# Output projection of a two-layer encoder trunk: a buffer of its own for y's weight sum, h's sum on a reloaded block, row sums of m1 and m2 put behind v's

## The chip, the cores and the metric

The kernel runs on one core of a Trainium2 chip. The metric is the device time of one execution in microseconds (us), the median of the timed runs. A second, profiled execution gives the trace; its times are counted from the start of its span.

## What is computed

Two layers, each a token mixer with three branches and then a feed-forward net (FFN), on 512 rows of width 1024 in float32. The change touches the output projection that closes the mixer and the layer norm behind it:

```
mix = jnp.einsum('bsd,de->bse', merged, w_out[l])            # 512x1024 by 1024x1024
x = _layer_norm(DEEPNORM_ALPHA * x + mix, ln1_g[l], ln1_b[l])
u = jnp.einsum('bsd,df->bsf', x, w_ffn_in[l])                # the FFN's first product
```

## The kernel before

**Products.** A float32 operand is carried as a pair of float32r parts, hi and lo. A product of two pairs takes three matmuls: hi by hi (L122), lo of one by hi (L123), hi by lo (L124). Weights are split after they are loaded: ScalarE (ACT) casts the hi part (L287 for a block of 128x2048; L154 for the FFN's and others' 128x1024), and VectorE (DVE) subtracts it from the loaded block to get lo (L288, L155).

**Seven products in place of eight.** The output projection is a Strassen-Winograd scheme on 512x512 blocks of `w_out`. Write W00, W01, W10, W11 for the blocks. Seven products, in the order m1, m2, y, v, x, g, h, use the weight blocks W00 (m1), W10 (m2), W00+W01 (y), W11 (v), W00+W01+W11 (x), W01+W11 (g) and W00+W01+W11+W10 (h). The left operands are sums of blocks of the merged activations (tiles `m1*`, `m2*`, `s12*`, `s43*`; L310, L311, L320 and L321 form them on DVE, L108 on ACT and L114 on DVE split them). `product` (L367) works one of them for two row tiles j = 0, 1 with 4 blocks k and 3 matmuls each: 24 matmuls of 128x512 each. x and g are added in PSUM onto m1's banks, h too, and v onto y's banks.

**Row sums.** The residual stream lies in tiles `z`, one for each row tile t and column half hf. `plus` (L1157) adds a finished PSUM bank to z on DVE: L1165 the first time (it scales z too), L1167 afterwards; with `final` it takes the statistics of the layer norm right behind it (L494). When both halves of a row tile have theirs, `normalise` follows: L511 and L513 on DVE, a power on GpSimd (POOL, L514), and L516 on DVE. Transposes on the TensorE (PE, L534 into `px`) turn z; ACT scales it (L550) and casts it (L106), DVE makes its lo part (L112), and the result `xT` feeds the FFN.

**Weight sums.** A load is a DMA of 1 MB issued from SyncE (SP, L174) into one of four staging buffers `st`. W00 is loaded into buffer `a` for m1. Behind m1's split an accumulating DMA (L178, issued from POOL) adds W01 onto `a`: y's block. For v, W11 is loaded into a buffer `d`, and DVE adds it onto `a` (L226): x's block. Behind x's split a second accumulating DMA adds W10 onto `a`: h's block. g's sum is made in a buffer `c` ahead of time, with an accumulating DMA of its own.

**What sets the order.** A list of items (L1215 to L1245) says in which order weight blocks are needed and which side work (`s_mleft`, `s_mright`, `s_turned`) goes with each. An item's weights are fetched up to three blocks ahead of its matmuls, since there are three buffers each for `wh` and `wl`. A tile scheduler then places each engine's instructions in one fixed order, and each engine works its own list strictly in that order. So does the DMA queue of SP. Both layers hold the same sequence here.

Of the kernel before, what the change touches and what calls it, by code (L numbers as in the profile page):

```python
# [56 lines left out]
def trunk(ctx, tc, x_in, xT_in, w_in, ret_norm_g, da_norm_g, lq1, lk1, lq2, lk2, w_a, w_b, w_c, b_merge, w_out,  # L57
          ln1_g, ln1_b, w_ffn_in, w_ffn_out, ln2_g, ln2_b, rel, rope_ret, rope_da, decay, out):
    nc = tc.nc
# [131 lines left out]
    class Chain(Halves):  # L191
# [12 lines left out]
        def y(self):  # L204
            return self.take(1, 1)

        def x(self):
            return self.take(1, 0)
# [4 lines left out]
        def v(self):  # L213
            return self.block(self.load(1, 1))

        def h(self):
            return self.block(self.__dict__.pop("a"))

    class Mixed(Chain):

        def v(self):
            self.d = self.load(1, 1)
            b = self.block(self.d)
            nc.vector.tensor_add(self.a, self.a, self.__dict__.pop("d"))  # L226
            return b

        def x(self):
            return self.take(1, 0)  # L230

        def y(self):
            return self.block(self.a)

    class Close(Halves):

# [130 lines left out]
    def product(acts, name, j, wt, ps=None):  # L367

        onto, sl = ps is not None, slice(P * j, P * j + P)
        ps = ps if onto else bank("pf")  # L370
        for k in range(wt.nk):
            hi, lo = acts[k].use[name]
            mm3(ps, hi[:, sl], lo[:, sl], wt.hi[:, k], wt.lo[:, k], k == 0 and not onto, k == wt.nk - 1, onto)
        return ps
# [257 lines left out]
    def layer(l):  # L632
# [7 lines left out]
        v = {}  # L640
# [421 lines left out]
        mq = {}  # L1062
# [32 lines left out]
        def u_branch(br, i):  # L1095
            w = (w_a, w_b, w_c)[br][l]
            nk = w.shape[0] // P

            def fn(wt):
                act = (oa, ob, oc)[br]  # L1100
                for j, d in enumerate(tiles(br, i)):
                    t = th.pop((br, d))
                    if br == 0:
                        away, t = t, g(name="th")
                        nc.sync.dma_start(t, away)
                    ps = proj_T(act, wt, P * j, nk=nk)
                    nc.vector.scalar_tensor_tensor(t, t, 1.0, ps, op0=ALU.add, op1=ALU.mult)
                    if br == 0:
                        acc[d] = t
                    else:  # L1110
                        nc.vector.tensor_add(acc[d], acc[d], t)
                    if br == 2 and j == 0:
                        q = mq[d] = Quarters()
                        pr = HalfPair("m1")
                        split(pr, acc[d][:, q.A], scale=0.5)
                        q.put("m1", pr, q.A)
                    elif br == 2:
                        pr = Pair("m2")
                        split(pr, acc[d], scale=0.5)
                        mq[d - 4].put("m2", pr, q.A)  # L1120
                        mq[d - 4].put("h", pr, q.B)
                    between()
            return [(cols_of(w, 0, br, i), nk)], fn
# [26 lines left out]
        x1 = {}  # L1150
# [9 lines left out]
        def plus(x, t, hf, ps, op, final=False):  # L1160

            z = x["z"][t][hf]
            if (t, hf) in x["fresh"]:
                x["fresh"].remove((t, hf))
                nc.vector.scalar_tensor_tensor(z, z, ALPHA, ps, op0=ALU.mult, op1=op)  # L1165
            else:
                nc.vector.tensor_tensor(z, z, ps, op=op)  # L1167
            if final:
                x["n"].stats(t, hf)
# [7 lines left out]

        def out_items():

            hv = Mixed(w_out[l], 0, 4)  # L1180
            w = {}

            def it(name, i, hf, op, last=False, whole=False):
                def fn(wt):
                    on = {"x": "m1", "g": "m1", "h": "m1", "v": "y"}.get(name, name)
                    for j in range(2):
                        t = 2 * i + j
                        w[on, j] = product(mq, name, j, wt, w.pop((on, j), None))
                        plus(x1, t, hf, w[on, j], op, last)
                        if name in ("m2", "v", "h"):  # L1190
                            w.pop((on, j))
                        if whole:
                            x1["n"].normalise(t)
                        between()
                return [getattr(hv, name)], fn

            add, sub = ALU.add, ALU.subtract
            return {"c": hv.ahead_c, "m1": it("m1", 0, 0, add), "m2": it("m2", 0, 0, add, True), "y": it("y", 1, 1, add),
                    "x": it("x", 0, 1, sub, True, True), "v": it("v", 0, 1, add), "g": it("g", 1, 1, sub, True),
                    "h": it("h", 1, 0, add, True, True)}  # L1200

        def s_turned(hf):
# [7 lines left out]
        o = out_items()  # L1210
# [15 lines left out]
        for (specs, fn), *groups in start + [  # L1226
            (w["x"], [p["a"]]), (u_gate(0, 3),), (w["g"],), (w["h"], [p["c"]]),
            (p["m1"], [s_dh(0)]), (p["y"], [], [s_r1(0)]), (p["v"], [s_dh(1)]), (p["m2"], [], [s_r1(1)]),
            (p["x"], [q["a"]]), (u_rqk(rq, RQ, 1),), (p["g"], [q["c"]]), (p["h"],),
            (q["m1"], [], [s_r2(0)]), (q["y"], [s_r2(1)]), (u_rqk(rk, RK, 1), [], [s_r3(0)]),  # L1230
            (q["v"], [s_dh(2)], [s_r3(1)]), (q["m2"], [], [s_r1(2)]), (q["x"], [s_dh(3)]), (u_cqk(0), [], [s_r1(3)]), (q["g"],), (q["h"],),
            (u_gate(2, 0), [s_r2(2)], [s_r2(3), s_r3(2)]), (u_cqk(1), [s_r3(3)] + c(0)[0], c(0)[1]),
            (u_branch(0, 0), c(1)[0] + [v_back(cv)], c(1)[1]), (u_branch(0, 1), *c(2)), (u_cqk(2), *c(3)),
            (u_branch(0, 2), *c(4)), (u_cqk(3), *c(5)), (u_branch(0, 3), *c(6)), 
            (u_dqk(0), [s_c3(5), s_c2(6)], [s_c1(7)]), (u_gate(1, 0), [s_c3(6)], [s_c2(7)]),
            (u_dqk(1), [v_back(dv), s_c3(7)] + d(0)[1]), (u_branch(1, 0), *d(1)),
            (u_gate(1, 1), [], d(2)[1]), (u_branch(1, 1), [s_d2(0)], d(3)[1]), (u_dqk(2), [s_d3(0)]),
            (u_gate(1, 2), *d(4)), (u_branch(1, 2), *d(5)), (u_dqk(3),),
            (u_gate(1, 3), *d(6)), (u_branch(1, 3), *d(7)), (u_gate(2, 1), [gates_in(2, 0), s_d4(2)], [s_d2(3)]),
            (u_gate(2, 2), [s_d3(3)], [rows_in, s_d4(3)]),  # L1240
            (u_branch(2, 0), [], [s_mleft(0)]), (u_branch(2, 1), [], [s_mleft(1)]), (u_gate(2, 3), [s_mright(0)], [s_mright(1)]),
            (u_branch(2, 2), [o["c"]]), (u_branch(2, 3), [], [s_mleft(2), s_mleft(3)]),
            (o["m1"], [s_mright(2)]), (o["m2"], [s_mright(3)]), (o["y"],), (o["v"],), (o["x"], [norm_rows]),
            (o["g"], [], [s_turned(0)]), (o["h"],),
        ]:  # L1245
            item(specs, fn, *groups)
# [237 lines left out]
```

## Time and profile before

| what | value |
|---|---|
| timed runs, median (lowest to highest) | 1887.76 us (1886.77 to 1888.65) |
| profiled execution, its own time | 1890.11 us |
| its span in the trace | 1888.3 us |
| PE busy | 1860.3 us, 99% of the span |
| DVE busy | 1392.3 us, 74% |
| ACT busy | 989.1 us, 52% |
| granted TensorE clock, mean | 0.996 |

The span is from the first instruction to the last; the execution's own time has 1.8 us around it. A row of the timeline gives the start, the length, the engine, the line and the operation, then what it writes and reads. A bracket at its end gives the idle time ahead of it on that engine and what ended it. Matmuls overlap: one of 128x512 is shown with 0.39 us, and the next starts 0.23 us later. The output projection lies at about 545 to 604 us in the first layer and 1486 to 1544 us in the second.

### The profile page before, as it was taken

Reading aid. Unit: us, or ns where it says so; the run is one execution under the profiler, and the core shown is the slowest. Engines: PE = TensorE matmul, PEld = TensorE weight load, DVE = VectorE, ACT = ScalarE, POOL = GpSimd, SP = SyncE. Lnnn points to the kernel's source line nnn. Section 1 sums busy time; section 2 is a strip of 40 time slices with the busy share of each in tenths; the row PEclk is TensorE's granted clock in tenths of the full one; section 3 lists DMA queues with packets and bytes.
Section 4 is the critical chain, followed back from the end, with each engine's and each line's share of the span. In section 5 each row is a group of like instructions: output and inputs, shape, how many; then the busy total and the mean of one; then the engine's idle time right before and its main releaser. Section 6 shows DMA issues by size and latency. Waiting matters only on the chain. (4 is left out here: it accounts for less than half of the span.)

```text
span 1888.3 us, 23317 instructions
## 1 busy us (share of the span) xinstructions
PE 1860.3 (99%) x8754; PEld 1547.7 (82%) x8754; DVE 1392.3 (74%) x2119; ACT 989.1 (52%) x1593; POOL 133.7 (7%) x151
## 2 busy tenths in 40 slices
PE   9999999999999999999999999999999999999998
PEld 7788888888877888788878888888888778888886
DVE  6777756677578776889587777567775887778886
ACT  5545545576544544555264555546665454455541
POOL 2000000000001000010020000000000011000100
PEclk9999999999999999999999999999999999999999
DMA  9585444232357677697486844533323576777871
GB/s 291 165 268 152 123 145 124 90 125 77 121 136 174 160 187 192 164 230 198 145 218 183 258 126 123 164 115 100 113 68 123 134 200 148 197 193 203 203 195 45
DMA packets 234881, 300.79 MB, mean 159 GB/s; under 512 B 8724, under 2 KB 127600, under 8 KB 234768
## 3 DMA queue, kind: packets, MB, share of 16 engines
q1 hardware_dynamic: 205488, 242.25, 39.3%
q0 software_dynamic: 29280, 57.05, 17.7%
q8 instruction: 69, 1.13, 0.3%
q14 instruction: 44, 0.36, 0.1%
HBM read 277.20 MB, written 22.07 MB: 158 GB/s over the span
## 5 line engine op out<-in xcount | busy, mean ns | idle before, releaser
L288 DVE TENSOR_TENSOR wl<-st,wh 128x2048 fp32r<-128x2048 f32 x140 | 320.1, 2289 | 124.2 <-ACT wh L287 123.6
L287 ACT CAST wh<-st 128x2048 fp32r<-128x2048 f32 x140 | 267.0, 1911 | 241.0 <-PE pf L124 112.0
L122 PE MATMUL pt<-xTh,wh 128*128 128x512 f32 x960 | 377.7, 394 | 2.5 <-ACT wh L154 1.6
L124 PE MATMUL pt<-xTh,wl 128*128 128x512 f32 x960 | 374.1, 390 | 0.0
L123 PE MATMUL pt<-xTl,wh 128*128 128x512 f32 x960 | 373.7, 389 | 0.0
L155 DVE TENSOR_TENSOR wl<-st,wh 128x1024 fp32r<-128x1024 f32 (+1 forms) x188 | 200.3, 1083 | 49.7 <-ACT wh L154 36.1
L154 ACT CAST wh<-st 128x1024 fp32r<-128x1024 f32 (+1 forms) x188 | 172.5, 940 | 107.3 <-PE pt L123 56.1
L122 PEld LDWEIGHTS pt<-xTh,wh 128*128 128x128 f32 x960 | 180.3, 188 | 40.1 <-ACT wh L154 2.5
L124 PEld LDWEIGHTS pt<-xTh,wl 128*128 128x128 f32 x960 | 180.2, 188 | 38.1
L123 PEld LDWEIGHTS pt<-xTl,wh 128*128 128x128 f32 x960 | 180.4, 188 | 36.2 <-DVE xTl L112 0.2
L122 PE MATMUL pf<-wh,xTh 128*128 128x512 f32 x336 | 133.3, 397 | 1.7 <-ACT rph L106 0.8
L123 PE MATMUL pf<-wl,xTh 128*128 128x512 f32 x336 | 132.0, 393 | 1.8 <-DVE wl L288 1.8
L124 PE MATMUL pf<-wh,xTl 128*128 128x512 f32 x336 | 131.5, 393 | 0.0
L123 PE MATMUL pf<-wl,s12h 128*128 128x512 f32 x256 | 100.0, 391 | 3.9 <-DVE wl L288 3.9
L122 PE MATMUL pf<-wh,s43h 128*128 128x512 f32 x256 | 101.1, 395 | 2.3 <-DVE z L1167 2.3
L123 PE MATMUL pf<-wl,s43h 128*128 128x512 f32 x256 | 101.1, 395 | 0.0
L124 PE MATMUL pf<-wh,s43l 128*128 128x512 f32 x256 | 100.9, 394 | 0.0
L122 PE MATMUL pf<-wh,s12h 128*128 128x512 f32 x256 | 100.2, 394 | 0.0
L124 PE MATMUL pf<-wh,s12l 128*128 128x512 f32 x256 | 99.4, 390 | 0.0
L762 ACT COPY tc<-pf 128x512 f32<-128x512 f32 x84 | 48.4, 589 | 82.9 <-PE pf L124 77.7
L122 PEld LDWEIGHTS pf<-wh,xTh 128*128 128x128 f32 x336 | 63.5, 189 | 18.3 <-ACT xf L550 1.6
L123 PEld LDWEIGHTS pf<-wl,xTh 128*128 128x128 f32 x336 | 63.5, 189 | 14.7 <-DVE wl L288 2.4
(328 smaller groups left out, 3665.8 us busy)
## 6 DMA issues: line engine op xcount, KB each, us to landing
st<-in_w_in SPq DMA_DIRECT2D x53, 1024.0 KB, 6.1
st<-in_w_ffn_in SPq DMA_DIRECT2D x38, 1024.0 KB, 5.6
st<-in_w_in SPq DMA_DIRECT2D x48, 512.0 KB, 5.1
st<-in_w_ffn_in POOLq DMA_DIRECT2D x20, 1024.0 KB, 10.0
st<-in_w_ffn_out SPq DMA_DIRECT2D x20, 1024.0 KB, 7.2
st<-in_w_ffn_out POOLq DMA_DIRECT2D x16, 1024.0 KB, 8.8
st<-in_w_in POOLq DMA_DIRECT2D x12, 1024.0 KB, 11.6
st<-in_w_ffn_in SPq DMA_DIRECT2D x24, 512.0 KB, 5.5
```

What stands on the lines that cost most here:

```text
L122: nc.tensor.matmul(ps, lh, rh, start=start, stop=False, skip_group_check=onto)
L123: nc.tensor.matmul(ps, lh, rl, start=False, stop=False, skip_group_check=onto)
L124: nc.tensor.matmul(ps, ll, rh, start=False, stop=stop, skip_group_check=onto)
L154: return [nc.scalar.copy(self.hi[:, a:b], self.st[:, a:b]), nc.vector.tensor_sub(self.lo[:, a:b], self.st[:, a:b], f(self.hi[:, a:b]))]
L155: nc.vector.tensor_sub(self.lo[:, a:b], self.st[:, a:b], f(self.hi[:, a:b]))]
L287: nc.scalar.copy(self.hi, st)
L288: nc.vector.tensor_sub(self.lo, st, f(self.hi))
L762: nc.scalar.copy(t[to, j], ps)
```

## The change

- y's block gets buffer `a` to itself: `ahead_a` loads W00 and adds W01 by an accumulating DMA, ahead of time (in the item u_branch(2, 0), five items before m1's). m1 loads W00 once more into a buffer of its own.
- x's block is made in v's buffer: DVE adds `a` onto `d` (L249 of the old file). It was `d` onto `a`.
- h's block is made on a freshly loaded W10, buffer `e`, to which DVE adds `d`. There is no accumulating DMA for it any more.
- `ahead_c` moves from u_branch(2, 2) to the item before it, behind `s_mright(1)`.
- The row sums of m1 and m2 are collected, and issued in v's item behind v's own row sum of the same j.

Per layer that is two more loads of 1 MB (six of `w_out` for four), one accumulating DMA less (two for three), and one DVE add of 128x2048 more (two for one). No matmul is added or removed. `Early`, which was there before for another product, takes the place of `Mixed`, which is removed; with it, every line behind it has a lower number in the changed file (16 less up to L1178).

```diff
--- before.py
+++ after.py
@@ -215,22 +215,6 @@
 
         def h(self):
             return self.block(self.__dict__.pop("a"))
-
-    class Mixed(Chain):
-
-
-
-        def v(self):
-            self.d = self.load(1, 1)
-            b = self.block(self.d)
-            nc.vector.tensor_add(self.a, self.a, self.__dict__.pop("d"))
-            return b
-
-        def x(self):
-            return self.take(1, 0)
-
-        def y(self):
-            return self.block(self.a)
 
     class Close(Halves):
 
@@ -1177,26 +1161,32 @@
 
         def out_items():
 
-            hv = Mixed(w_out[l], 0, 4)
+            hv = Early(w_out[l], 0, 4)
             w = {}
+            late = []
 
             def it(name, i, hf, op, last=False, whole=False):
                 def fn(wt):
                     on = {"x": "m1", "g": "m1", "h": "m1", "v": "y"}.get(name, name)
                     for j in range(2):
                         t = 2 * i + j
-                        w[on, j] = product(mq, name, j, wt, w.pop((on, j), None))
-                        plus(x1, t, hf, w[on, j], op, last)
-                        if name in ("m2", "v", "h"):
-                            w.pop((on, j))
+                        ps = w[on, j] = product(mq, name, j, wt, w.pop((on, j), None))
+                        add = functools.partial(plus, x1, t, hf, ps, op, last)
+                        if name in ("m1", "m2"):
+                            late.append(add)
+                        else:
+                            add()
+                        if name == "v":
+                            for fn in late[j::2]:
+                                fn()
                         if whole:
                             x1["n"].normalise(t)
                         between()
                 return [getattr(hv, name)], fn
 
             add, sub = ALU.add, ALU.subtract
-            return {"c": hv.ahead_c, "m1": it("m1", 0, 0, add), "m2": it("m2", 0, 0, add, True), "y": it("y", 1, 1, add),
-                    "x": it("x", 0, 1, sub, True, True), "v": it("v", 0, 1, add), "g": it("g", 1, 1, sub, True),
+            return {"c": hv.ahead_c, "a": hv.ahead_a, "m1": it("m1", 0, 0, add), "m2": it("m2", 0, 0, add, True),
+                    "y": it("y", 1, 1, add), "x": it("x", 0, 1, sub, True, True), "v": it("v", 0, 1, add), "g": it("g", 1, 1, sub, True),
                     "h": it("h", 1, 0, add, True, True)}
 
         def s_turned(hf):
@@ -1238,8 +1228,8 @@
             (u_gate(1, 2), *d(4)), (u_branch(1, 2), *d(5)), (u_dqk(3),),
             (u_gate(1, 3), *d(6)), (u_branch(1, 3), *d(7)), (u_gate(2, 1), [gates_in(2, 0), s_d4(2)], [s_d2(3)]),
             (u_gate(2, 2), [s_d3(3)], [rows_in, s_d4(3)]),
-            (u_branch(2, 0), [], [s_mleft(0)]), (u_branch(2, 1), [], [s_mleft(1)]), (u_gate(2, 3), [s_mright(0)], [s_mright(1)]),
-            (u_branch(2, 2), [o["c"]]), (u_branch(2, 3), [], [s_mleft(2), s_mleft(3)]),
+            (u_branch(2, 0), [o["a"]], [s_mleft(0)]), (u_branch(2, 1), [], [s_mleft(1)]), (u_gate(2, 3), [s_mright(0)], [s_mright(1), o["c"]]),
+            (u_branch(2, 2),), (u_branch(2, 3), [], [s_mleft(2), s_mleft(3)]),
             (o["m1"], [s_mright(2)]), (o["m2"], [s_mright(3)]), (o["y"],), (o["v"],), (o["x"], [norm_rows]),
             (o["g"], [], [s_turned(0)]), (o["h"],),
         ]:
```

The class that is used now, as it stands in both files:

```
    class Close(Halves):
        def ahead_a(self):
            self.a = self.load(0, 0)
            self.more(self.a, 0, 1)
        def m1(self):
            return self.block(self.load(0, 0))
        def v(self):
            self.d = self.load(1, 1)
            b = self.block(self.d)
            nc.vector.tensor_add(self.d, self.d, self.__dict__.pop("a"))
            return b
...
        def y(self):
            return self.block(self.a)
        def x(self):
            return self.block(self.__dict__.pop("d"))
        def h(self):
            return self.block(self.__dict__.pop("e"))

    class Early(Close):
        def m2(self):
            return self.block(self.load(1, 0))
        def x(self):
            b = self.block(self.d)
            self.e = self.load(1, 0)
            nc.vector.tensor_add(self.e, self.e, self.__dict__.pop("d"))
            return b
```

Three places show what it moves in the engines' lists (first layer; the second has the same). The first is DVE from v's split to x's split, before. `wl_5144` is v's lo part and `wl_5186` x's; `st_4998` is `a`, `st_5141` is `d`; `pf_5148` and `pf_5170` hold m2.

```order
L288 TENSOR_TENSOR wl_5144<-st_5141,wh_5143 128x2048
L114 SCALAR_TENSOR_TENSOR s12l_5092<-sa_5088,s12h_5091 128x512
L310 TENSOR_TENSOR sa_5095<-th_2584,th_3156 128x256
L226 TENSOR_TENSOR st_4998<-st_4998,st_5141 128x2048
L311 TENSOR_TENSOR sa_5095<-sa_5095,th_2584 128x256
L1167 TENSOR_TENSOR z_4786<-z_4786,pf_5148 128x512
L1167 TENSOR_TENSOR z_4788<-z_4788,pf_5170 128x512
L494 BN_STATS bn_4802<-z_4786 128x6
L494 BN_STATS bn_4803<-z_4788 128x6
L114 SCALAR_TENSOR_TENSOR s12l_5099<-sa_5095,s12h_5098 128x512
L320 TENSOR_TENSOR sb_5120<-th_3081,sa_5088 128x256
L321 TENSOR_TENSOR sb_5120<-th_2509 128x256
L288 TENSOR_TENSOR wl_5186<-st_4998,wh_5185 128x2048
```

The same place in the changed kernel, where `wl_5144` is v's, `wl_5182` x's, `st_4842` is `a`, `st_5141` is `d` and `st_5185` is `e`.

```order
L272 TENSOR_TENSOR wl_5144<-st_5141,wh_5143 128x2048
L114 SCALAR_TENSOR_TENSOR s12l_5094<-sa_5090,s12h_5093 128x512
L294 TENSOR_TENSOR sa_5097<-th_2584,th_3156 128x256
L233 TENSOR_TENSOR st_5141<-st_5141,st_4842 128x2048
L295 TENSOR_TENSOR sa_5097<-sa_5097,th_2584 128x256
L260 TENSOR_TENSOR st_5185<-st_5185,st_5141 128x2048
L114 SCALAR_TENSOR_TENSOR s12l_5101<-sa_5097,s12h_5100 128x512
L304 TENSOR_TENSOR sb_5121<-th_3081,sa_5090 128x256
L305 TENSOR_TENSOR sb_5121<-th_2509 128x256
L272 TENSOR_TENSOR wl_5182<-st_5141,wh_5181 128x2048
```

Between the two splits, m2's two row sums and their statistics have gone, and the add that makes h's block (L260, 128x2048) has come in behind the one that makes x's.

The second place is DVE around h's split, before. `wl_5219` is g's lo part, `wl_5249` h's, made from `st_4998`, the buffer `a`; `pf_5106` and `pf_5127` hold m1 with x on it (g and h come on later), `pf_5190` and `pf_5204` y with v.

```order
L288 TENSOR_TENSOR wl_5219<-st_5023,wh_5218 128x2048
L114 SCALAR_TENSOR_TENSOR s43l_5167<-sb_5163,s43h_5166 128x512
L1165 SCALAR_TENSOR_TENSOR z_4787<-z_4787,pf_5190 128x512
L1165 SCALAR_TENSOR_TENSOR z_4789<-z_4789,pf_5204 128x512
L1167 TENSOR_TENSOR z_4787<-z_4787,pf_5106 128x512
L288 TENSOR_TENSOR wl_5249<-st_4998,wh_5248 128x2048
L494 BN_STATS bn_4802<-z_4787 128x6
L1167 TENSOR_TENSOR z_4789<-z_4789,pf_5127 128x512
L511 BN_AGGR mv_5266<-bn_4802 128x2
```

And the changed kernel from g's split to that of the first FFN block: `wl_5217` is g's, `wl_5253` h's, made from `st_5185`, which is `e`, and `wl_5309` the first FFN block's. `pf_5148` and `pf_5168` hold m2, `pf_5108` and `pf_5128` m1 with x on it, and `pf_5188` and `pf_5202` y with v.

```order
L272 TENSOR_TENSOR wl_5217<-st_5001,wh_5216 128x2048
L1149 SCALAR_TENSOR_TENSOR z_4787<-z_4787,pf_5188 128x512
L1151 TENSOR_TENSOR z_4786<-z_4786,pf_5148 128x512
L1151 TENSOR_TENSOR z_4788<-z_4788,pf_5168 128x512
L478 BN_STATS bn_4802<-z_4786 128x6
L1149 SCALAR_TENSOR_TENSOR z_4789<-z_4789,pf_5202 128x512
L478 BN_STATS bn_4803<-z_4788 128x6
L1151 TENSOR_TENSOR z_4787<-z_4787,pf_5108 128x512
L272 TENSOR_TENSOR wl_5253<-st_5185,wh_5252 128x2048
L478 BN_STATS bn_4802<-z_4787 128x6
L1151 TENSOR_TENSOR z_4789<-z_4789,pf_5128 128x512
L495 BN_AGGR mv_5270<-bn_4802 128x2
L272 TENSOR_TENSOR wl_5309<-st_5306,wh_5308 128x2048
```

m2's two row sums and their statistics stand between v's and x's row sums now, so that x's first one (onto `z_4787`) and h's split come later in the list than they did, and h's split is made from a buffer that DVE itself completed.

The third place is PE where g ends and h begins (`m2h` and `m2l` are h's left operand), before: the first four transposes (L534) stand ahead of h's first matmul.

```order
L122 MATMUL pf_5127<-wh_5218,s43h_5166 128x512
L123 MATMUL pf_5127<-wl_5219,s43h_5166 128x512
L124 MATMUL pf_5127<-wh_5218,s43l_5167 128x512
L534 MATMUL px_5337<-ident_75,z_4786 128x128
L534 MATMUL px_5354<-ident_75,z_4786 128x128
L534 MATMUL px_5371<-ident_75,z_4787 128x128
L534 MATMUL px_5388<-ident_75,z_4787 128x128
L122 MATMUL pf_5106<-wh_5248,m2h_4857 128x512
L123 MATMUL pf_5106<-wl_5249,m2h_4857 128x512
```

In the changed kernel the transposes stand behind the matmuls of h, j = 1: all of them among h's last three.

```order
L123 MATMUL pf_5128<-wl_5253,m2h_5043 128x512
L124 MATMUL pf_5128<-wh_5252,m2l_5044 128x512
L518 MATMUL px_5341<-ident_75,z_4786 128x128
L518 MATMUL px_5358<-ident_75,z_4786 128x128
L122 MATMUL pf_5128<-wh_5252,m2h_5086 128x512
L518 MATMUL px_5375<-ident_75,z_4787 128x128
L518 MATMUL px_5392<-ident_75,z_4787 128x128
L123 MATMUL pf_5128<-wl_5253,m2h_5086 128x512
L518 MATMUL px_5341<-ident_75,z_4788 128x128
L518 MATMUL px_5341<-ident_75,z_4786 128x128
```

## The prediction

> **What bounds the kernel now.** I read the page's busy shares, then PE's waits, the timelines around each, and the windows for the granted clock.
>
> ```profile
> PE 1860.3 (99%) x8754; PEld 1547.7 (82%) x8754; DVE 1392.3 (74%) x2119; ACT 989.1 (52%) x1593; POOL 133.7 (7%) x151
> ```
>
> PE is the bound and keeps all its matmuls. So the change can be worth only what PE waits, or works slowly, in the output projections: the waits from 530 to 640 us (first layer), then from 1480 to 1600 us (second).
>
> ```profile
> PE pf L122 <- DVE z L1167: 2.3, 1, 2.3
> PE pf L123 <- DVE wl L288: 2.0, 1, 2.0
> PE pf L122 <- ACT m L108: 2.0, 1, 2.0
> ```
>
> ```profile
> PE pf L123 <- DVE wl L288: 2.0, 1, 2.0
> PE pf L122 <- ACT m L108: 1.8, 1, 1.8
> PE px L534 <- DVE z L516: 0.9, 1, 0.9
> PE pf L122 <- DVE rs L513: 0.3, 1, 0.3
> ```
>
> In the order of time I call them stall 1 (`m`), stall 2 (x's `wl`) and stall 3 (`z`; in the second layer the transposes `px`). On PE, first layer:
>
> ```profile
> 556.74 0.39 PE L124 MATMUL pf<-wh,m 128*128 128x512 f32 x1
> 559.10 0.50 PE L122 MATMUL pf<-wh,m 128*128 128x512 f32 x1 [1.97 <-ACT m L108]
> 559.43 0.40 PE L123 MATMUL pf<-wl,m 128*128 128x512 f32 x1
> ...
> 575.82 0.50 PE L123 MATMUL pf<-wl,s12h 128*128 128x512 f32 x1 [1.97 <-DVE wl L288]
> ...
> 588.69 0.39 PE L123 MATMUL pf<-wl,s43h 128*128 128x512 f32 x1
> 588.91 0.39 PE L124 MATMUL pf<-wh,s43l 128*128 128x512 f32 x1
> 591.64 0.50 PE L122 MATMUL pf<-wh,s43h 128*128 128x512 f32 x1 [2.34 <-DVE z L1167]
> ...
> 594.07 0.63 PE L123 MATMUL pf<-wl,s43h 128*128 128x512 f32 x1
> 594.50 0.63 PE L124 MATMUL pf<-wh,s43l 128*128 128x512 f32 x1
> ```
>
> Normally a matmul starts 0.23 us after the one before (588.69 to 588.91), and the first after a stall 0.33 (559.10 to 559.43). Stall 1 thus costs 559.10 - 556.74 - 0.23 + 0.10 = 2.23 us and stall 3, by the same sum, 2.60. Behind stall 3 the step is 0.43 us (594.07 to 594.50): half speed. The windows view shows where (its columns after the busy times are the granted clock, the DMA share and GB/s):
>
> ```profile
> 574.00:577.00 3.00, 1.18 (x5) 1.00 (x6) 2.97 (x3) 2.36 (x2) 0.69 (x1) 1.00 0.91 257
> 592.00:596.00 4.00, 4.00 (x12) 3.12 (x11) 3.54 (x5) 0.00 (x0) 3.55 (x2) 0.57 0.91 253
> 1516.00:1521.00 5.00, 4.45 (x12) 3.49 (x13) 4.97 (x7) 1.73 (x3) 1.28 (x1) 0.66 0.83 219
> ```
>
> With c the share of a window at half clock, 1 - c/2 = 0.57 over 4 us gives 3.4 us, and 0.66 over 5 us the same: 3.4 us at half speed cost **1.7 us**. The first follows stall 3 of the first layer, the second stall 2 (1.97 us) of the second layer. An equal stall 2 of the first layer is followed by none (1.00 in the first row). So of two alike, one is punished.
>
> **The change part by part.** *Stall 1 goes.* ACT, first layer:
>
> ```profile
> 556.83 1.90 ACT L287 CAST wh<-st 128x2048 fp32r<-128x2048 f32 x1 [5.25 <-DMA st<-in_w_out]
> 558.63 0.41 ACT L108 ACTIVATE m<-th 128x256 fp32r<-128x256 f32 x1
> ...
> 586.16 3.72 ACT L287 CAST wh<-st 128x2048 fp32r<-128x2048 f32 x2 [7.73 <-DMA st<-in_w_out]
> ```
>
> The cast of y's block (556.83) waits for the accumulating DMA, and the cast of `m` that PE needs is queued behind it. Now the sum is made long before. By my walk (the rows' durations, in the changed order) the cast starts when an old `wh` buffer is free, at 554.3, and `m` ends at 556.6, before PE comes to it at 556.97. Gain 2.23; in the second layer 1.77 + 0.16 + 0.10 = 2.03. Next late is stall 2.
>
> *Stall 2 stays.* DVE between v's and x's split:
>
> ```profile
> 567.30 2.28 DVE L226 TENSOR_TENSOR st<-st 128x2048 f32<-128x2048 f32 x1
> ...
> 569.83 1.28 DVE L1167 TENSOR_TENSOR z<-z,pf 128x512 f32<-128x512 f32 x2
> 571.03 1.28 DVE L494 BATCH_NORM_STATS2 bn<-z 128x6 f32<-128x512 f32 x2
> ...
> 573.49 2.28 DVE L288 TENSOR_TENSOR wl<-st,wh 128x2048 fp32r<-128x2048 f32 x1
> ```
>
> The late sums of m2 take away 569.83 to 572.23, that is 2.40 us. The new add for h's block (128x2048, priced by L226's row: 2.28) comes into the same queue ahead of x's split. Net -0.12. As PE and DVE both come about 2.2 us earlier, the wait stays near 1.95 us. Behind x's split the new add would not have held it.
>
> *Stall 3 goes, first layer.* The `wh` cast of h at 586.16 waits for the accumulating DMA, and DVE's split behind it blocks the row sum that PE waits for:
>
> ```profile
> 588.10 2.29 DVE L288 TENSOR_TENSOR wl<-st,wh 128x2048 fp32r<-128x2048 f32 x1 [3.29 <-ACT wh L287]
> ...
> 590.91 0.67 DVE L1167 TENSOR_TENSOR z<-z,pf 128x512 f32<-128x512 f32 x1
> ```
>
> Now `e` is complete when DVE has added, about 569.8. h's cast starts at 581.3 by the walk and DVE comes to h's split at 583.25, the row sum to 586.06, and PE wants it at 586.7: the stall falls to about 0.06. Gain 2.60 - 0.06 = 2.54 and the half clock behind it, 1.70. In the second layer the transposes' wait goes:
>
> ```profile
> 1535.29 0.99 PE L534 MATMUL px<-ident,z 128*128 128x128 f32 x4 [0.94 <-DVE z L516]
> ```
>
> It costs 0.94 + 0.17 to the end of the matmul before, and these four take 0.99 where the first layer's took 0.60 (596.09, below): 1.50. The half clock behind stall 2 goes too, and is put back below as a chance: 1.70.
>
> *A new wait at h.* g's first row sum stands behind the first FFN block's split (2.28 us, as x's) and is read by h's first matmul: 590.4 by the walk, against 589.5 for PE. That is 0.86 + 0.10, where before 0.24 + 0.10 were lost (0.32 + 0.10 in the second layer). Loss 0.62 and 0.54.
>
> *The FFN's start.* It comes about 6 us earlier on PE, but the transposes come later relative to it: at the end of h and not at its start.
>
> ```profile
> 596.09 0.60 PE L534 MATMUL px<-ident,z 128*128 128x128 f32 x4
> ...
> 603.87 0.39 PE L122 MATMUL pf<-wh,xTh 128*128 128x512 f32 x1
> ...
> 617.01 0.39 PE L122 MATMUL pt<-xTh,wh 128*128 128x512 f32 x1
> ```
>
> ```profile
> 600.08 0.57 ACT L550 ACTIVATE xf<-px,colv 128x256 f32<-128x256 f32 x1 [1.85 <-PE px L534]
> 600.68 0.41 ACT L106 CAST xTh<-xf 128x256 fp32r<-128x256 f32 x1
> 600.99 0.56 ACT L550 ACTIVATE xf<-px,colv 128x256 f32<-128x256 f32 x1
> ...
> 604.07 1.06 ACT L154 CAST wh<-st 128x1024 fp32r<-128x1024 f32 x1 [0.70 <-PE pf L124]
> ```
>
> Before, 20.9 us lie between the first transposes and the first `pt` row, 4.8 of them h's matmuls (21 x 0.2267) that now come ahead. ACT turns a piece of `xT` in 0.91 us (600.08 to 600.99). Some 13 pieces, four casts of 1.05 and two copies are its work up to that row, 11.8 + 4.2 + 1.1 = 17.1 us. My walk has the first transposes at 595.3, so the row would come at 612.4; by PE's work alone at 597.8 + 13.14 = 610.9. I take 1.6 us given back per layer. The bounds: nothing (PE sets it) and 4.8 (all 16 pieces and the casts before that row: 595.3 + 0.6 + 14.6 + 4.2 + 1.1 = 615.8).
>
> *The loads.* Per layer two more of 1 MB on SP's queue; the landing times of the staging loads here are:
>
> ```profile
> DMA to landing us min/median/max: 4.0/6.3/9.7
> ```
>
> Two of four `st` buffers hold `a` and `c`. So m1's new load can issue only when the split of the item before has read its buffer, at 534.7 by the walk, and lands by 538.7 to 544.4. Its cast was at 543.54, so 0 to 0.9 us late, in most cases not at all; I take 0. `e` issues at 553.8 and lands by 563.5 at the latest, against 567.6 when DVE wants it: hidden. `a` and `c` are ready 40 and 10 us before they are read. POOL's issue of the DMA that is gone was waited for by nobody.
>
> **Sum.** First layer 2.23 + 2.54 + 1.70 - 0.62 - 1.6 = 4.25. Second layer 2.03 + 1.70 + 1.50 - 0.54 - 1.6 = 3.09. Together 7.34, with no half clock behind the two stalls 2 that stay. Of two such, one was punished above; so I expect one, 1.70, and a saving of 5.6 us. From the profiled 1890.11 (span 1888.3, 1.8 around it) that leads to 1884.5; the timed median is 2.35 lower, with the same waits by assumption: 1887.76 - 5.6 = **1882.2**.
>
> [...]
>
> **Rivals.** *No half clock behind the stalls that stay*: 1887.76 - 7.34 = 1880.4. For it, one of two had none. [...] *Both punished*: 7.34 - 3.4 = 3.9, 1883.8. Against it, that row.
>
> *The gain is given back at the FFN's start*: if ACT does all 16 pieces first, 4.8 is lost per layer and not 1.6, and 7.34 - 6.4 - 1.7 leaves about 0, **1887.8**; halfway, 1885. For it, ACT's 17.1 us of work from 595.3 on against PE's 13.1 from 597.8. Against it, the order leaves FFN matmuls between the pieces. That the change doesn't do what it says (h's or y's cast still waiting for a DMA) would end there too; the loads above speak against it.
>
> *Slower*: m1's reload. To eat 5.6 us and end 0.2% (3.8 us) above, m1 would have to be 4.7 us late in each layer, its load landing at 543.5 + 4.7 = 548.2, that is 13.5 us after its issue. Nothing here took over 9.7. At that 9.7 the price is 0.9 per layer, 1884.0.
>
> **Chances.** A measurement of this kernel tells about 0.2%, 3.8 us, from no change. Forecast, one half clock (1881 to 1883.5) 0.43; none (1880.4 or less) 0.18; both, or m1 late (1884) 0.14, half of it over the bound; gain given back (1885 to 1889) 0.19; slower 0.06. Faster 0.43 + 0.18 + 0.07 = 0.68; the same 0.07 + 0.19 = 0.26; slower 0.06. The range goes from 1879.0 (no half clock, and 1.4 us of the FFN's loss not there) to 1886.5 (most of the gain given back).
>
> **What would show it.** Right: no wait of PE for `m` at L108 and none over 0.3 us for `z` in g; y's and h's ACT casts with no wait for a DMA; the wait for x's `wl` still 1.8 to 2.1 us; a wait of 0.5 to 1.2 us at h's first matmul; the first `pt` row of the FFN 55 to 57 us behind the last matmul before stall 1's place. Wrong: PE waiting at `m1` for a cast that waits for `st`; waits over 1 us for `xTh` or `px`; DVE idle ahead of the add for h's block, which would mean that `e` is late; or stall 2 gone or over 2.5 us.

## The result and the profile after

The changed kernel takes **1878.72 us** (median of 4 runs, 1878.23 to 1879.94). The runs of the kernel before beside it have a median of 1888.2; the ratio is 0.9951, 95% interval 0.9934 to 0.9969. A second comparison ("The changed kernel, once more", below) gave 1878.88 beside 1886.75, ratio 0.9962 (0.9947 to 0.9976). So it is faster, by about 7 to 9 us; the forecast was 5.6 us and 1882.2, and the measured time lies 0.3 us below the range. Here, with lower line numbers, are the page's busy shares and PE's waits of the changed kernel, first layer, then second.

```profile
PE 1858.0 (99%) x8754; PEld 1544.6 (82%) x8754; DVE 1396.5 (74%) x2121; ACT 989.3 (53%) x1593; POOL 127.1 (7%) x149
```

```profile
PE pf L123 <- DVE wl L272: 1.9, 1, 1.9
PE pf L122 <- DVE mv L495: 0.6, 1, 0.6
PE pf L122 <- ACT xf L534: 0.4, 2, 0.3
```

```profile
PE pf L123 <- DVE wl L272: 2.0, 1, 2.0
PE pf L122 <- DVE mv L495: 0.6, 1, 0.6
PE pf L122 <- ACT xf L534: 0.4, 2, 0.3
```

Stalls 1 and 3 are gone from both lists, stall 2 is left as it was, and a wait of 0.6 us at h has come. ACT's casts of y's and h's blocks no longer wait for a DMA:

```profile
553.94 1.91 ACT L271 CAST wh<-st 128x2048 fp32r<-128x2048 f32 x1 [2.69 <-issue]
555.82 0.42 ACT L108 ACTIVATE m<-th 128x256 fp32r<-128x256 f32 x1
...
582.66 1.92 ACT L271 CAST wh<-st 128x2048 fp32r<-128x2048 f32 x1 [7.59 <-PE pf L124]
```

On DVE the add for h's block (L260) stands ahead of x's split (L272):

```profile
567.24 2.28 DVE L260 TENSOR_TENSOR st<-st 128x2048 f32<-128x2048 f32 x1
569.57 0.69 DVE L114 SCALAR_TENSOR_TENSOR s12l<-sa,s12h 128x512 fp32r<-128x512 f32 x1
570.18 0.42 DVE L304 TENSOR_TENSOR sb<-th,sa 128x256 f32<-128x256 f32 x1
570.51 0.42 DVE L305 TENSOR_TENSOR sb<-th 128x256 f32<-128x256 f32 x1
570.85 2.29 DVE L272 TENSOR_TENSOR wl<-st,wh 128x2048 fp32r<-128x2048 f32 x1
```

And on PE the wait for that split, the wait at h, the FFN's first row and its first `pt` row:

```profile
573.19 0.50 PE L123 MATMUL pf<-wl,s12h 128*128 128x512 f32 x1 [1.95 <-DVE wl L272]
...
591.76 0.47 PE L122 MATMUL pf<-wh,m2h 128*128 128x512 f32 x1 [0.56 <-DVE mv L495]
...
599.10 0.50 PE L122 MATMUL pf<-wh,xTh 128*128 128x512 f32 x1
...
613.90 0.39 PE L122 MATMUL pt<-xTh,wh 128*128 128x512 f32 x1
```

**Where the time went.** The program falls into stretches: up to m1's first matmul (the first row `pf<-wh,m`), from there to the FFN's first row (`pf<-wh,xTh`), from there to its first `pt` row, and so on. These are the starts of those rows, taken from the two profiled executions (us):

| stretch | before | changed | difference |
|---|---|---|---|
| start to m1, first layer | 554.25 | 553.92 | -0.33 |
| m1 to FFN | 49.62 | 45.18 | -4.44 |
| FFN to `pt` | 13.14 | 14.80 | +1.66 |
| `pt` to m1 of the second layer | 878.18 | 874.46 | -3.72 |
| m1 to FFN, second layer | 48.33 | 43.62 | -4.71 |
| FFN to `pt` | 13.17 | 14.79 | +1.62 |
| `pt` to the last matmul | 322.47 | 322.47 | 0.00 |

The four stretches that the change touches, from m1 to `pt` in both layers, give 5.87 us against 5.6 forecast. In them the kernel before has two half clocks (granted clock at half for 3.41 us), the changed kernel one. A further 3.72 us come from a place that the change doesn't touch: a wait in the first layer's FFN of the kernel before (1.83 us) with a half clock behind it (1.7 us). Its rows are on PE, ACT, POOL and SP, in this order:

```profile
758.89 0.50 PE L123 MATMUL pf<-wl,xTh 128*128 128x512 f32 x1 [1.83 <-DVE wl L288]
```

```profile
754.60 1.91 ACT L287 CAST wh<-st 128x2048 fp32r<-128x2048 f32 x1 [4.54 <-DMA st<-in_w_ffn_in]
```

```profile
744.32 1.28 POOL L178 DMA_DIRECT2D st<-in_w_ffn_in  x1 [10.56 <-DMA st<-in_w_ffn_in]
```

```profile
745.07 0.37 SPq L174 DMA_DIRECT2D st<-in_w_ffn_in  x1
```

The load issued at 745.07, 0.75 us behind an accumulating DMA, took 9.4 us to land. In the changed kernel the same load is issued at 741.96, ahead of that DMA (742.78 on POOL), and took 5.8, and its cast waits 0.89 and not 4.54 us:

```profile
747.84 1.91 ACT L271 CAST wh<-st 128x2048 fp32r<-128x2048 f32 x1 [0.89 <-DMA st<-in_w_ffn_in]
```

### The profile page after: what moved, and what is told of

Its sections match the earlier page's. It is cut to its first block, busy times and chain, and to the rows that moved or that the text cites. A ratio compares the mean times of both kernels' runs of the same rounds, so it can differ in the third digit from the quotient of the medians.

```text
span 1878.2 us, 23320 instructions
## 1 busy us (share of the span) xinstructions
PE 1858.0 (99%) x8754; PEld 1544.6 (82%) x8754; DVE 1396.5 (74%) x2121; ACT 989.3 (53%) x1593; POOL 127.1 (7%) x149
## 5 line engine op out<-in xcount | busy, mean ns | idle before, releaser
L272 DVE TENSOR_TENSOR wl<-st,wh 128x2048 fp32r<-128x2048 f32 x140 | 320.2, 2290 | 117.9 <-ACT wh L271 116.4
L124 PEld LDWEIGHTS pf<-wh,xTl 128*128 128x128 f32 x336 | 62.6, 188 | 15.3 <-DVE xTl L112 2.3
```

The source lines that it names most:

```text
L124: nc.tensor.matmul(ps, ll, rh, start=False, stop=stop, skip_group_check=onto)
L272: nc.vector.tensor_sub(self.lo, st, f(self.hi))
```

## The experiments

All times are medians beside runs of the kernel before in the same comparison. There were three comparisons: the first four experiments (median before 1886.32); "One more DVE operation", "The add for h on GpSimd" and "No weight sum on DVE" (1886.37, on another chip); the other four (1886.75). The ratio is the recorded one and not the quotient of the two medians; gains across comparisons are taken from it. The first four start from the kernel before, the others from the changed kernel, except where an earlier experiment is named.

### The kernel before, once more

No edit.

> The kernel before, unchanged, once more. Against the profile before, the changed kernel also lost a wait that no step of the prediction named: 1.83 us at 758.9 us in the first layer's FFN (pf L123 waiting for the wl of L288) with a half clock of 1.7 us behind it; the stretch from the FFN's first pt row to the second layer's m1 went from 878.18 to 874.46 us. Theory A (a tie between two DMAs: an accumulating DMA issued just ahead of a load that is needed soon, decided anew in each execution): the wait is there in some executions and not in others, so this profile may be without it and then has about 874.6 us in that stretch. Theory B (the order of the DMAs in this kernel makes it): the wait is there again, 1.8 us at the same place, and the stretch again has 878 us. Time: 1888.2 within 1.5 us by both.

1885.09 us, ratio 0.9998 (0.9988 to 1.0007). The stretch from `pt` to the second layer's m1 is 874.36 us, and PE's only wait from 640 to 960 us is this:

```profile
PE pf L122 <- ACT xTh L106: 0.3, 1, 0.3
```

Theory A holds: with the same order of instructions, the FFN's wait came in one execution and not in another. In all other profiles the stretch has 874.3 to 874.5 too. So the 3.72 us aren't the change's. It isn't enough that the load stands behind the DMA: here it is issued 0.1 us behind it (743.61 and 743.51) and lands in 5.65 us. In the thirteen profiles this load lands in 5.6 to 6.1 us where it is issued at most 0.23 us behind the DMA or ahead of it, in 7.1 at 0.64 us behind, and in 9.4 at 0.75 us. So the distance of the two goes with the wait, though no experiment set it. The two rows here, POOL's and SP's:

```profile
743.51 1.28 POOL L178 DMA_DIRECT2D st<-in_w_ffn_in  x1 [10.87 <-DMA st<-in_w_ffn_in]
```

```profile
743.61 0.37 SPq L174 DMA_DIRECT2D st<-in_w_ffn_in  x1
```

### The row sums alone

```diff
-                        plus(x1, t, hf, w[on, j], op, last)
+                        add = functools.partial(plus, x1, t, hf, ps, op, last)
+                        if name in ("m1", "m2"):
+                            late.append(add)
...
+                        if name == "v":
+                            for fn in late[j::2]:
+                                fn()
```

> The kernel before with only the row sums of m1 and m2 put behind v's. Here the order has the add that makes x's block right behind y's split and no row sum of m2 ahead of x's split. Theory 1 (these sums stood on DVE's path to x's split): stall 2 goes in both layers, 2.07 each and the half clock of the second layer, 1.7: 5.8 us less, 1882.4; stalls 1 and 3 stay, stall 3 perhaps shorter, since h's accumulating DMA starts earlier. Rival (the sums only stand where DVE has to wait anyway; the gain is all from the buffers): 1888 within 1 us, stall 2 still 1.9 us.

1881.14 us, 0.9975 (0.9966 to 0.9985): 4.7 us less by the ratio. The first theory holds for stall 2; it had stall 3 stay. First layer, then second:

```profile
PE pf L122 <- ACT m L108: 1.8, 1, 1.8
PE pf L122 <- ACT xf L550: 0.4, 2, 0.3
PE pf L122 <- DVE mv L511: 0.3, 1, 0.3
PE pf L122 <- DVE z L1165: 0.2, 1, 0.2
```

```profile
PE pf L122 <- ACT m L108: 1.6, 1, 1.6
PE pf L122 <- DVE mv L511: 0.6, 1, 0.6
PE pf L122 <- ACT xf L550: 0.4, 2, 0.2
PE pf L122 <- DVE z L1165: 0.2, 1, 0.2
```

Stall 1 stays, stall 2 is gone, and so is stall 3, though h's block is still made by an accumulating DMA: that DMA is issued at 573.4 and not at 576.3, since x's split is earlier, and the sums behind it are not held up by h's cast any more. The sums alone take away two stalls of three.

### y's own buffer alone

```diff
-    class Mixed(Chain):
+    class Own(Close):                 # ahead_a, m1, v, y as in Close; m2 as in Early
...
+        def x(self):
+            b = self.block(self.d)
+            self.more(self.d, 1, 0)
+            return b
+        def h(self):
+            return self.block(self.__dict__.pop("d"))
...
```

The list of items is that of the changed kernel (`ahead_a` five items before m1, `ahead_c` one item earlier).

> The kernel before with y's block in a buffer of its own (a loaded early, m1 loaded again, x's block made on v's buffer), but h's block by an accumulating DMA onto it and the row sums where they were. Theory 1 (three separate waits): only stall 1 goes, 2.23 and 2.03 us, 1884.0; stall 2 stays at 1.9, stall 3 at 2.3 (first layer), and half clocks fall as they fall, 1.7 each. Rival (the early load does most of it, the rest follows): stalls 2 and 3 shrink by over 1 us too, 1880 or less.

1881.85 us, 0.9982 (0.9973 to 0.9992): 3.4 us by the ratio, where 4.2 were expected. Stall 1 is gone, stall 2 is 2.0, and stall 3 is still 1.9 us (first layer) and 1.1, with another 1.0 at the transposes (second layer): three separate waits.

### The reload for h alone

```diff
         def x(self):
-            return self.take(1, 0)
+            b = self.block(self.a)
+            self.e = self.load(1, 0)
+            nc.vector.tensor_add(self.e, self.e, self.__dict__.pop("a"))
+            return b
+        def h(self):
+            return self.block(self.__dict__.pop("e"))
```

> The kernel before with only h's block made on a reloaded W10 (an add of 2.28 us on DVE in place of the accumulating DMA); y's block by accumulating DMA and the row sums as before. The order has the new add behind x's split. Theory 1: stall 3 goes, 2.5 us in the first layer and 1.5 in the second, less about 0.6 each for a new wait at h, and with it the half clock of the first layer: 3 to 5 us less, 1883 to 1885; stalls 1 and 2 stay. Rival (the DVE add costs as much as the DMA's wait saved): 1887 to 1889, a wait of 2 us in its place at g or h.

1884.96 us, 0.9995 (0.9986 to 1.0004): no gain that can be told, and the rival holds. Stall 3 is replaced by a wait at h's first matmul:

```profile
595.12 0.47 PE L122 MATMUL pf<-wh,m2h 128*128 128x512 f32 x1 [1.73 <-DVE rs L517]
```

### The changed kernel, once more

No edit.

> The changed kernel once more, beside the kernel before on one chip. The profiles so far give it 1876.5 us of span with no half clock behind its two stalls 2, and 1.7 us more for each; the kernel before has 1881.0 with none, and waits near 1.8 us in four to six places. Theory C (a wait of 1.95 us is punished only if nearly all of it falls into one 3.4 us window, so about one time in two): times from 1878.3 (none) over 1880.0 (one) to 1881.7 (two), median 1879 to 1880, some 7 us less than the kernel before. Theory D (the 9.5 us seen at first are all the change's): 1876.5 to 1877.5 beside a median before of 1886.3.

1878.88 us, 0.9962 (0.9947 to 0.9976), from 1877.82 to 1881.63. By the ratio 7.2 us, as theory C has it, and not 9.5. The profiled run, 1877.82 us, has stall 2 twice and no half clock at all. DVE is busy nearly the whole time from m1 to the FFN:

```profile
553.60:597.20 43.60, 41.08 (x186) 32.71 (x184) 42.84 (x57) 17.66 (x16) 2.42 (x3) 1.00 0.62 174
```

That is 42.84 of 43.60 us (the third busy time). The kernel before had 41.87 of 49.70:

```profile
554.20:603.90 49.70, 43.17 (x186) 33.92 (x186) 41.87 (x59) 19.49 (x20) 5.77 (x4) 0.97 0.65 160
```

### The changed kernel with its row sums at once

```diff
-                        if name in ("m1", "m2"):
-                            late.append(add)
-                        else:
-                            add()
...
+                        plus(x1, t, hf, w[on, j], op, last)
...
```

> The changed kernel with the row sums of m1 and m2 taken at once, as before. The order then has the add for h's block behind x's split, where the row sums had held its place. Theory 1 (one place in DVE's queue, taken by the one or the other): stall 2 stays at 1.9 to 2.1 us, a wait of about 1.7 at h as in the kernel with only the reload, in place of 0.56; about 0.7 us more per layer, 1.4 us above the changed kernel. Rival (the late sums take 2.4 us off the path in each layer): stall 2 of 4.3 us, 5 us or more above the changed kernel.

1881.4 us, 0.9974 (0.9963 to 0.9984), 2.5 us above the changed kernel. Stall 2 stays at 2.0 us and the wait at h is 1.7: the first theory's waits. The add for h and the row sums had only changed places. Without its half clock the profile has 0.9 us more from m1 to `pt` in both layers together; where the rest of the 2.5 lies isn't shown.

```profile
PE pf L123 <- DVE wl L272: 2.0, 1, 2.0
PE pf L122 <- DVE rs L497: 1.7, 1, 1.7
PE px L518 <- DVE z L500: 0.5, 1, 0.5
```

### The add for h behind x's split

```diff
+            self.e = self.load(1, 0)
             b = self.block(self.d)
-            self.e = self.load(1, 0)
-            nc.vector.tensor_add(self.e, self.e, self.__dict__.pop("d"))
+            add = nc.vector.tensor_add(self.e, self.e, self.__dict__.pop("d"))
+            tc.add_manual_dep(add.ins, b.sub.ins.name, ...)      # behind x's split
```

The load of `e` is also written ahead of x's block now.

> The changed kernel with the add for h's block pinned behind x's split on DVE. Theory 1 (that add alone makes the stall 2 that is left): x's split starts when its cast ends, 1.8 us sooner; stall 2 falls to 0.2 us in both layers and no half clock is left behind it: 3.6 us less and on average 1.7 more, 5 us below the changed kernel; the wait at h may grow by up to 0.5. Rival (another piece of DVE's queue takes the place): stall 2 still over 1 us, less than 2 us gained.

1879.8 us, 0.9964 (0.9951 to 0.9977): nothing gained, and my theory fell.

```profile
571.85 0.50 PE L123 MATMUL pf<-wl,s12h 128*128 128x512 f32 x1 [0.60 <-DVE wl L282]
...
590.59 0.47 PE L122 MATMUL pf<-wh,m2h 128*128 128x512 f32 x1 [1.39 <-DVE rs L507]
```

Stall 2 fell to 0.60 us, and the wait at h grew to 1.39, with another of 0.4 at g. From m1 to the FFN it takes 43.58 us, the 43.57 of the changed kernel's second profile. In that time DVE is busy 42.80 us. So I formed theory E: DVE is the bound here, and a wait that is moved only comes back.

### One more DVE operation

```diff
             tc.add_manual_dep(add.ins, b.sub.ins.name, ...)
+            nc.vector.tensor_tensor(self.e, self.e, self.e, op=ALU.max)
```

It starts from the kernel with the add behind x's split.

> The kernel with the add for h's block pinned behind x's split, and behind that add one more DVE operation of the same size (the maximum of e with itself, 2.28 us), off the way to x's split. Theory E (from v's split to h DVE itself is the bound: it was busy 42.8 of the 43.6 us there, and moving the add only moved the wait): the stretch from m1's first matmul to the FFN's first row grows by 2.0 to 2.3 us in each layer, 4.4 us above the kernel without the extra operation, more with a half clock. Theory 1 (only the one wait for x's split is on the path, the rest of DVE's queue has slack): under 1 us in all.

1884.65 us, 0.9987 (0.9975 to 0.9998): by the ratios 4.3 us above the kernel without the operation. The wait is at g now, 3.8 us in both layers, each time with half clock behind it:

```profile
PE pf L122 <- DVE z L1162: 3.8, 1, 3.8
PE pf L123 <- DVE wl L283: 0.6, 1, 0.6
```

From m1 to the FFN the layers take 48.80 and 47.63 us. The half clock costs 1.7 in the second and 3.0 in the first layer (two windows long there, 6.1 us of it with work). Without it 45.8 and 45.9 are left, 2.2 and 2.4 more than without the operation: all of the 2.28 us. Theory E holds for this stretch. But from the FFN's first row to `pt` it takes 13.25 us and not 14.8, so 1.5 of it comes back, and m1 to `pt` is only 0.7 and 0.8 us longer. Most of the 4.3 us is half clock; that theory E had named 4.4 is luck.

### h's block by an accumulating DMA, the rest as changed

```diff
         def x(self):
             b = self.block(self.d)
-            self.e = self.load(1, 0)
-            nc.vector.tensor_add(self.e, self.e, self.__dict__.pop("d"))
+            self.more(self.d, 1, 0)
             return b
...
```

h's block is then `d` (in the changed kernel `e`).

> The changed kernel with h's block made by an accumulating DMA onto v's buffer behind x's split, so without the reload of W10 and without its DVE add; y's own buffer and the late row sums stay. Theory 1 (the late sums and not the reload take stall 3 away): stall 2 falls to 0.2 us, the DMA starts at about 571.5 and lands by 581.5, ahead of h's cast at 582.7, so no wait comes in its place: 5 us below the changed kernel. Rival (the accumulating DMA's wait at h is what the reload saved): stall 3 back with 1.5 to 2.3 us and half clocks behind it, level with the changed kernel or above.

**1876.6 us**, 0.9949 (0.9934 to 0.9964), 2.3 us below the changed kernel in the same comparison. It is the fastest kernel here, though the two intervals overlap. First layer:

```profile
PE pf L122 <- DVE mv L508: 0.8, 1, 0.8
PE pf L122 <- DVE rs L510: 0.7, 1, 0.7
PE pf L123 <- DVE wl L285: 0.6, 1, 0.6
PE px L531 <- DVE z L513: 0.3, 1, 0.3
```

No wait is over 0.8 us, and no half clock follows one. The gain is half of what I expected: DVE has 2.28 us less to do, yet the waits that are left add up to 2.4 us. From m1 to `pt` it takes 57.53 and 57.16 us, where the changed kernel's second profile has 58.36 and 58.39. The gain doesn't lie where theory E had it: m1 to the FFN takes 44.37 and 44.03 us, more than the 43.57 and 43.61 there, and the FFN to `pt` 13.15 and 13.13 in place of 14.8. So DVE's work sets the first stretch when work is added, but taking 2.28 us off didn't shorten it.

### The add for h on GpSimd

```diff
-            nc.vector.tensor_add(self.e, self.e, self.__dict__.pop("d"))
+            nc.gpsimd.tensor_add(self.e, self.e, self.__dict__.pop("d"))
```

> The changed kernel with the add for h's block on GpSimd in place of DVE; buffers, loads and late row sums as in the changed kernel. Theory E (DVE is the bound of the stretch): 2.28 us less work for DVE; the kernel without that add and with an accumulating DMA in its place gained 0.85 us per layer with the FFN's start counted, and so should this, 1876.6 to 1877.5, with no wait of 1.9 us for x's split. Rival (GpSimd's add slows DVE, or takes so long that h's cast waits): a wait of over 1 us at h or g, or DVE's operations longer than 2.29 us while it runs; 1879 or more.

1883.87 us, 0.9984 (0.9974 to 0.9993), by the ratios 4 us above the changed kernel: the rival. POOL, then DVE:

```profile
567.42 4.65 POOL L268 TENSOR_TENSOR st<-st 128x2048 f32<-128x2048 f32 x1 [35.69 <-DVE st L233]
```

```profile
569.33 4.88 DVE L280 TENSOR_TENSOR wl<-st,wh 128x2048 fp32r<-128x2048 f32 x1
```

x's split took 4.88 us and not 2.29 while GpSimd's add ran, and stall 2 grew to 3.2 us.

### No weight sum on DVE

```diff
-            hv = Early(w_out[l], 0, 4)
+            hv = Apart(w_out[l], 0, 4)
...
+    class Apart(Chain):
+        def ahead_a(self):
+            self.a = self.load(0, 0)
+            self.more(self.a, 0, 1)
+        def m1(self):
+            return self.block(self.load(0, 0))
```

`Chain` has the rest: y's and x's splits are each followed by an accumulating DMA onto `a`, and v's block is a load of its own.

> The changed kernel with no weight sum on DVE at all: buffer a of y takes W11 by an accumulating DMA behind y's split (x's block) and W10 by another behind x's split (h's block); m1's and v's blocks are loads of their own, and the row sums stay late. Theory E: DVE has 4.6 us less per layer than in the changed kernel, but x's cast must now wait for a DMA issued at about 559 that lands by 568 to 569: stall 2 of 1 to 1.6 us comes back, and h's DMA lands by 582 to 583. Level with the kernel with one accumulating DMA, 1876 to 1878. Rival (DMA waits are what matters): 1880 or more, with waits of 2 us at x and h.

1878.98 us, 0.9958 (0.9943 to 0.9973), level with the changed kernel, between the 1876 to 1878 of theory E and the 1880 of the rival. The wait, forecast at 1 to 1.6 us, is 3.29 us in the first layer and 2.6 in the second, and of stall 1's kind: x's cast waits for the DMA until 568.24, and the cast of `s12h` is queued behind it.

```profile
570.72 0.50 PE L122 MATMUL pf<-wh,s12h 128*128 128x512 f32 x1 [3.29 <-ACT s12h L108]
```

## Why the prediction was right in its steps and wrong in its number

- *Stall 1 goes*: shown. The cast of `m` ended at 556.2, and PE has no wait there.
- *Stall 2 stays*: shown. 1.95 and 1.96 us were measured where 1.95 was forecast, with L260 ahead of the split. That the add alone holds it was half the truth: behind the split it costs as much at h.
- *Stall 3 goes*: shown, but the cause given, the reload, is neither enough nor needed. Alone it only moves the wait to h and gains nothing, and the late row sums alone remove stall 3 too. In the changed kernel the DMA's wait is traded for 2.28 us of DVE, which is busy 98% of this stretch.
- *A new wait at h*: 0.56 and 0.58 us, forecast 0.86.
- *The FFN's start*: 1.66 and 1.62 us given back, forecast 1.6. The experiments agree, with the first sixteen transposes: about 14.8 us where all stand at the end of h (the changed kernel, the late sums alone, the pinned add), 14.3 where four stand ahead of h and twelve at its end (the reload alone, the row sums at once), 13.1 to 13.3 where all are done by about the middle of h (the others).
- *The sum*: the prediction puts m1 to `pt` without half clock at 62.76 - 4.25 = 58.51 and 61.50 - 3.09 = 58.41 us. The changed kernel's second profile has 58.36 and 58.39.
- *The signs*: all that were named for right came. The first `pt` row stood 55.9 us behind the matmul ahead of stall 1's place in the second profile, and 57.5 in the first, with the half clock between.
- *A rival's sum*: 7.34 - 6.4 - 1.7 is -0.8 and not "about 0", so that rival's time was 1888.5. Nothing hangs on it.

The parts can be set side by side by the time from m1 to `pt`, both layers together, with 1.7 us taken off for each half clock:

| kernel | m1 to `pt`, both layers | against the kernel before, once more |
|---|---|---|
| before: first profile, once more | 120.9, 121.2 | |
| the reload for h alone | 121.4 | +0.2 |
| y's own buffer alone | 117.6 | -3.6 |
| the row sums alone | 116.8 | -4.4 |
| the change: first profile, once more | 116.7, 116.8 | -4.4 |
| h's block by an accumulating DMA, the rest as changed | 114.7 | -6.5 |

So the waits that went are worth 4.4 us, where the prediction without half clocks has 7.34 - 3.4 = 3.9. In these stretches the row sums alone do as much as the whole change, though their timed median lies 2.3 us higher, which the profile doesn't explain. The medians of all runs differ by more than the waits, 7.7 us. The rest would be mostly half clocks, as an estimate: these stretches of the kernel before hold two and one of them, those of the changed kernel one and none.

The step that failed is the last one of the sum: "so I expect one, 1.70, and a saving of 5.6 us", and "with the same waits by assumption". Two things were wrong in it. First, the run in the middle has no half clock. The profiled run without any took 1877.82 us and the median of the eight runs of the changed kernel is 1878.7. The first profiled run, at 1879.94 us, held the one half clock of the forecast, by luck. The mean granted clock tells the same: it is 0.999 in the three profiles without a half clock in the layers and 0.998 or less in all others, and five of the eight runs have 0.999. The rival without half clock, 7.34 us, is what the second comparison measured (7.2). Second, the base. The three timed runs had a median of 1887.76, while that of the 67 runs of the kernel before in all comparisons is 1886.4 (1884.3 to 1891.9); whether that is chance or the chip isn't shown. And the profiled execution held a wait that came in one of the kernel's two profiles and that I had not looked for, since it lies outside the change's stretches; whether the three timed runs held it can't be seen. 1887.76 is 1.4 us above the longer median, and the half clock is 1.7; together 3.1 of the 3.5 us by which the forecast missed. The range's lower end of 1879.0 had put the missing time at the FFN's start, which cost what was forecast.

Why one half clock in two was too many: in these runs it depended on where the wait fell. In the records of the granted clock, half speed always started on a grid of 3.41 us within an execution, and ended on it, but for the one at the program's end. In the kernel before it starts at 592.53, 759.78 and 1517.54 us, 49 and 222 times 3.413 us apart, and each time lasts 3.41 us. Two waits of the same length in the kernel with the add on GpSimd show it, first layer and second. The first wait, 3.20 us, falls into two windows, 1.74 and 1.46 us of it, the second, 3.19, into one for 2.9 us. The windows view right behind them:

```profile
574.50:578.50 4.00, 4.00 (x18) 3.12 (x18) 3.67 (x7) 2.44 (x2) 0.00 (x0) 1.00 0.72 252
1508.00:1512.00 4.00, 3.64 (x10) 2.89 (x11) 3.10 (x7) 1.06 (x1) 0.00 (x0) 0.57 0.61 197
```

The first is not punished, the second is. Over all profiles, waits with up to 1.78 us in one window were not punished, two of five from 1.80 to 1.85 were, and all from 1.93 on (so were one window with a wait of 0.98 us among transposes, and one with the last 0.75 us of a wait of 3.8, already at half clock). So in these profiles a wait of about 1.95 us was punished only if nearly all of it fell into one window. The changed kernel's first profile shows both: the whole 1.95 us of the first layer's wait lie in one window, and half clock follows at 574.37; the second layer's wait of 1.96 lies, by the grid, with 0.54 and 1.42 us in two, and none follows. Of the sixteen waits of 1.94 to 2.00 us six were followed by half clock, so by this count two such waits bring 0.75 on average, and none or one are both likely.

## What to carry to other kernels

When a wait is removed, look at how busy the engine behind it is in that stretch and not over the whole kernel: DVE, 74% over the span, was at 98% in the output projection once the DMA waits were gone, and from then on moving its work only moved the wait, while taking 2.28 us off it brought 0.8 and 1.2 us in the two layers, by way of the transposes at the FFN's start. Test each part of a change alone: here two parts made all of the gain, and the third cost 2.3 us. And look through the profiled execution for waits outside the change that may be there by chance, and take the time before from many runs, before a saving of 0.3% is subtracted from it.

## What the runs showed of the hardware

GpSimd's add of 128x2048 took 4.65 us, DVE's 2.28, and a DVE split beside it 4.88 in place of 2.29. It overlapped the add for 2.74 us and took 2.59 longer: the two ran as if one after the other. Not every DVE operation was held up: the row sums from PSUM and a statistics operation beside the same add (567.52 to 569.40) took their usual time, 1.28 us for two sums, as in the kernel before (569.83), and 0.68 for the statistics, where one behind the add (576.70) took 0.69. Why the split was held up and these were not, no run here shows. In the kernel with one more DVE operation, a wait of 3.8 us brought two windows of half clock in a row in one layer and one in the other.
